# First stage of a two-layer backbone on one core: another split of the low halves between VectorE and GpSimd, other modulation pages, another order at the stage's end

## The chip, the core and the metric

The kernel runs on one core of a Trainium2 chip. The core has a matmul engine (TensorE, PE in the profile; its weight loads are listed as PEld), three engines for elementwise work (VectorE = DVE, ScalarE = ACT, GpSimd = POOL), a queue processor for loads (SyncE = SP) and 16 DMA engines. The metric is the device time of one execution in microseconds; smaller is better. The kernel before was timed three times: 1805.2, 1808.09 and 1814.19 us, median 1808.09.

## The reference, cut to what matters

Two layers work on 1024 latent tokens of width 1024, with 256 context tokens beside them: first windowed attention with 16 query heads and 4 key/value heads, then a Conformer convolution module. The change touches the start of the first layer only: the modulation vectors, the norm, and the first projections of the attention layer.

```python
shift, scale, gate = jnp.split((silu_c @ ada_w[i] + ada_b[i])[:, None, :], 3, axis=-1)
h_lat = modulate(rmsnorm(x, norm_g[i]), shift, scale)
shift_c, scale_c, gate_c = jnp.split(silu_cc @ ada_w[i] + ada_b[i], 3, axis=-1)
h_ctx = modulate(rmsnorm(h_ctx_stream, norm_g[i]), shift_c, scale_c)
...
proj = h_lat @ w_in
q = apply_rope(split_heads(proj[..., :q_end], N_Q_HEADS), cos, sin)
k = apply_rope(split_heads(proj[..., q_end:k_end], N_KV_HEADS), cos, sin)
v = split_heads(proj[..., k_end:v_end], N_KV_HEADS)
z = proj[..., v_end:]
kv_c = h_ctx @ w_in[:, q_end:v_end]
y = (o * jax.nn.silu(z)) @ w_out
```

## The kernel before

**Products.** An fp32 product A*B is made of three matmuls on rounded halves: high*high, low*high, high*low. A high half is a copy that ACT rounds, a low half is a subtraction (`split_lo`) on DVE or POOL. For weights the halves are called whi and wlo, made from the loaded page wraw; for the modulated latent tokens hh and hl, made from hf; for the context hch and hcl; for the modulation matrix ahi and alo, made from araw.

**The first stage** is written out instruction by instruction. `x` comes in as eight row tiles of 128 tokens, in two halves (`xs0`, `xs1`). ACT squares a row tile (`square`), `normalise` scales it on the engines that are listed, PE transposes it by 128 columns (`turn`), and `x_tiles` scales and shifts the result into hf and splits it. `x_mm(kt, half, acc, which)` multiplies the column tile `kt` of one half of the tokens by the weight chunks in `which` (0 = k, 1 = q of the first head, 2 = v), into PSUM. `acc0` and `acc1` are these sums for the two halves of the tokens; the third of `acc0` (v) and the first of `acc1` (k) are the two halves of one PSUM tile, `sb`. `c_tile` does for a context column tile what `turn` and `x_tiles` do for a latent one. `idle` issues matmuls of zeros.

**Modulation.** The modulation matrix is worked off in four blocks of four pages, `ada_load`, `ada_split`, `ada_mm` and `ada_cols` in this order. The pages in `ADA_FP` are multiplied in fp32 by the vector `cf`, without a split (in the profile one row of four passes, x4, for a page); the others as halves by `c4`, four matmuls. `ADA_G` names the pages whose low half POOL makes; the rest are DVE's. `ada_mm` copies the block's row to `arow`, and `ada_cols` turns it into the columns `mod` that `x_tiles` needs.

**Weights.** `WStream` loads chunks of 128 columns ahead into wraw; `wsA.split()` rounds the next one on ACT and subtracts on the engine that `lo_eng` gives. Chunk 3 is z, the gate of the first head.

**Order.** Each engine works through its own queue. While `pin("PVAG")` holds, PE, DVE, ACT and POOL keep the order of the program; after `pin("P")` only PE does, and the other engines' instructions are placed by the scheduler. Before the change, `pin("P")` stands at the very end of the stage, behind the ropes of both halves (`rope_start`: a copy on ACT, two DMAs on ACT's queue that swap the halves, a product on DVE; `rope_end`: a product on POOL, a sum on DVE, the rounded copy on ACT, the low half on POOL), the copy of v (`finish`), the context products (`gemm_ctx`) and the rounding of chunk 3. Then z's projection and the next q are put into a queue (`enqueue`), from which `fill(n)` issues n matmuls, and the attention begins.

All instructions of the engines are recorded by one helper, line 90, so the profile's rows are told apart by the names of their tiles.

Of the kernel before, what the change touches and what calls it, by code (L numbers as in the profile page):

```python
# [14 lines left out]
P = 128  # L15
# [17 lines left out]
ADA_FP = ((0, 0), (0, 1), (0, 2), (0, 3), (1, 3))  # L33
ADA_G = ((1, 0), (1, 1), (2, 0), (2, 1), (3, 0), (3, 1))
# [61 lines left out]
def backbone_kernel(  # L96
# [18 lines left out]
    pg = Pages(pgpool, 45, "page", 1024)  # L115
# [13 lines left out]
    def ps_o(i=None):  # L129
        if i is None:  # L130
            oflip[0] ^= 1
            i = oflip[0]
        return ps.tile([P, 512], F32, tag=f"o{i}", name=nm("pso"), bufs=1)
# [125 lines left out]
    chunks = []  # L259
# [15 lines left out]
    wsA = WStream(chunks, nraw=4, lo_eng=lambda i: V if i == 3 else G)  # L275
# [46 lines left out]
    def idle(n):  # L322
        o = sb[:, 512:1024]
        for _ in range(n):
            PE.matmul(o, zr[:, 0:P], zr, start=True, stop=True)
# [4 lines left out]
    tp = ps_g()  # L330
# [53 lines left out]
    def ada_split(pr, pages=range(4)):  # L384
        for i in pages:
            if (pr, i) not in ADA_FP:
                eng = G if (pr, i) in ADA_G else V
                raw = araw[pr][i]
                rv = raw.rearrange("p a b c -> p a (b c)")
                h, l = pg.alloc(F32R, [2, 512], "ahi"), pg.alloc(F32R, [2, 512], "alo")  # L390
                act(h, rv, AF.Copy)
                split_lo(eng, l, rv, h)
                pg.free(raw)
                araw[pr][i] = (h, l)

    ada_o = {}

    def ada_mm(pr, pages=range(4)):

        if 0 in pages:  # L400
            ada_o[pr] = ps_o(0)
        o = ada_o[pr]
        for i in pages:
            for k in range(2):
                if (pr, i) in ADA_FP:
                    r = araw[pr][i].rearrange("p a b c -> p a (b c)")
                    parts = [(cf, r)]
                else:
                    parts = [(c4, r) for r in araw[pr][i]]
                for n, (c, r) in enumerate(parts):  # L410
                    PE.matmul(o[0:4], c[:, 2 * i + k, :], r[:, k], start=i + k + n == 0,
                              stop=i + k == 4 and n == len(parts) - 1)
            pg.free(*(araw[pr][i] if len(parts) == 2 else (araw[pr][i],)))
        if 3 in pages:
            V.tensor_copy(R[pr][0:4, 0:512], o[0:4])

    def ada_cols(pr):

        rw, m = R.pop(pr), mods[pr]
        cps = ps_o(1)  # L420
        for i in range(4):
            PE.matmul(cps[:, 2 * i:2 * i + 2], rw[0:5, i * P:(i + 1) * P], sel[0:5], start=True, stop=True)
        hp.free(rw)
        with tc.high_priority():
            V.tensor_copy(m[:, 0:2], cps[:, 0:4].rearrange("p (a b) -> p a b", b=2))
            for i in range(2):
                V.tensor_scalar(out=m[:, 2 + i], in0=cps[:, 4 + 2 * i:6 + 2 * i], scalar1=1.0,
                                scalar2=vt[:, 96 + 2 * pr + i:97 + 2 * pr + i], op0=ALU.add, op1=ALU.mult)
# [53 lines left out]
    ada_mm(0, range(4))  # L482
    tps = [turn(xs0, kt, ps_g) for kt in range(2)]
    wsA.split()
# [4 lines left out]
    ada_split(1, range(2))  # L489
    x_tiles((tps[0], 0, 0, V), (tps[1], 1, 0, V))  # L490
    ada_split(1, range(2, 4))
# [5 lines left out]
    ada_mm(1)  # L497
# [7 lines left out]
    normalise(xs1, (V, A, V, V), lambda: x_tiles((tps[0], 2, 0, V), (tps[1], 3, 0, G)))  # L505
    idle(2)
    x_mm(2, 0, acc0, range(3))
    x_mm(3, 0, acc0, range(3))
    ada_split(2, range(2))
    tps = [turn(xs1, kt, ps_g) for kt in (0, 1)] + [turn(xs1, 2, lambda: ps_o(1))]  # L510
    ada_mm(2, range(1))
    x_tiles((tps[0], 0, 1, V), (tps[1], 1, 1, G))
    x_tiles((tps[2], 2, 1, V))
    ada_split(2, range(2, 4))
# [4 lines left out]
    t3 = turn(xs1, 3, lambda: ps_o(1))  # L519
    x_tiles((t3, 3, 1, G))  # L520
    ada_mm(2, range(1, 2))
    x_mm(1, 1, acc1, range(3))
    ada_mm(2, range(2, 4))
    x_mm(2, 1, acc1, range(3))
    ada_cols(2)
    tp = turn(xs0, 4, lambda: ps_o(0))
    x_mm(3, 1, acc1, (0,))
    tq = turn(xs1, 4, lambda: ps_o(1))
    x_tiles((tp, 4, 0, V), (tq, 4, 1, G))
    x_mm(3, 1, acc1, (1, 2))  # L530
    ada_split(3, range(2))
    tp = turn(xs0, 5, lambda: ps_o(0))
    tq = turn(xs1, 5, lambda: ps_o(1))
    x_tiles((tp, 5, 0, V), (tq, 5, 1, G))
# [8 lines left out]
    ada_mm(3)  # L543
    c_tile(ctodo.popleft(), 1)
    x_mm(5, 0, acc0, range(3))
    ada_cols(3)
    tp = turn(xs0, 6, lambda: ps_o(0))
    x_mm(5, 1, acc1, (0,))
    tq = turn(xs0, 7, lambda: ps_o(1))
    x_tiles((tp, 6, 0, V), (tq, 7, 0, G))  # L550
# [3 lines left out]
    tq = turn(xs1, 7, lambda: ps_o(1))  # L554
    x_mm(6, 0, acc0, range(3))
    x_tiles((tp, 6, 1, V), (tq, 7, 1, G))
    pg.free(*xs1)
    wsA.load()
# [8 lines left out]
    x_mm(7, 1, acc1, (0,))  # L567
    c_tile(ctodo.popleft(), 1)
    x_mm(7, 1, acc1, (1, 2))
# [518 lines left out]
    tails = [finish("v", 0, 0, acc0[2], d0[2])]  # L1088
    o = ps_o(0)
    run(gemm_ctx(wsA.hl[0], o))  # L1090
    rope_end(rk0, lo, *(t[:, lo] for t in d0[0]), V)
    finish("k", 0, 2, o, d0[0])
    rope_end(rq0, lo, *(t[:, lo] for t in d0[1]), V)
    o = ps_o(1)
    run(gemm_ctx(wsA.hl[2], o))
    rk1, rq1 = rope_start(acc1[0], hi), rope_start(acc1[1], hi, pg)
    tails.append(finish("v", 0, 1, acc1[2], d0[2]))
    tails.append(finish("v", 0, 2, o, d0[2]))
    rope_end(rk1, hi, *(t[:, hi] for t in d0[0]), V)
    rope_end(rq1, hi, *(t[:, hi] for t in d0[1]), V)  # L1100
    wsA.split()
# [4 lines left out]
    pin("P")  # L1106
# [3 lines left out]
    fill(8)  # L1110
    tails[0]()
    fill(8)
# [628 lines left out]
```

## Time and profile before

| | us |
|---|---|
| runs | 1805.2, 1808.09, 1814.19 |
| profiled execution | 1804.66 |
| its span on the core | 1802.9 |

The page gives the busy time of each engine and its share of the span. The views that the prediction reads are the windows (busy time of each engine in a stretch, then the granted clock of PE, the DMA share and GB/s), the waits (what PE waited for, with the total, the number and the longest), and the timeline (start, length, engine, line, operation, output<-inputs, and in brackets the idle time before with its releaser). Names of buffers stand without their numbers there. The second view of the page divides the span into 40 slices of 45 us and shows PE's busy share and clock in tenths:

```profile
PE   8859999989998999999999999999999999999997
PEclk9979999999999999999999999999999999999999
```

The first three slices are the stage of the change and its end; nearly all that follows has a nine.

### The profile page before, as it was taken

How to read it: one execution, taken by the hardware profiler on the slowest of the kernel's cores; microseconds unless marked ns; L12 is line 12 of the kernel's file. 1: busy time of each engine (PE TensorE's matmuls, PEld its weight loads, DVE VectorE, ACT ScalarE, POOL GpSimd, SP SyncE). 2: the span in 40 equal slices, each digit the busy share in tenths (PEclk: the TensorE clock that was granted, in tenths of full speed). 3: DMA queues.
4: the chain of work that ended last, by engine and by line, in shares of the span. 5: the costliest groups of instructions: out<-in, count | busy, mean ns of one | idle time of the engine just before them, and what ended most of it. 6: DMA issues, size and time to landing. Idle time of an engine off the chain costs nothing.

```text
span 1802.9 us, 23880 instructions
## 1 busy us (share of the span) xinstructions
PE 1736.4 (96%) x8418; PEld 1430.2 (79%) x8418; DVE 1144.6 (63%) x2063; ACT 864.0 (48%) x1407; POOL 952.2 (53%) x853
## 2 busy tenths in 40 slices
PE   8859999989998999999999999999999999999997
PEld 4648887878887888878888888888888888788886
DVE  4735564546634564546613339999999999967823
ACT  5434443444433453444623436665656565366731
POOL 3544666356645665554200137999988888131300
PEclk9979999999999999999999999999999999999999
DMA  9123443445423443324886643111020202376971
GB/s 325 60 71 89 148 143 86 121 122 158 129 85 120 146 146 105 122 86 135 292 281 236 237 133 99 54 35 48 24 88 30 82 30 72 111 252 224 338 270 47
DMA packets 195324, 242.45 MB, mean 134 GB/s; under 512 B 11798, under 2 KB 126790, under 8 KB 195204
## 3 DMA queue, kind: packets, MB, share of 16 engines
q1 hardware_dynamic: 188340, 230.09, 39.1%
q10 hardware_dynamic: 6864, 10.84, 2.6%
q8 instruction: 66, 1.08, 0.3%
q14 instruction: 54, 0.44, 0.1%
HBM read 188.70 MB, written 41.69 MB: 128 GB/s over the span
## 4 chain that ended last, share of the span: by engine, by line
PE 85%; DMA 5%; POOL 3%; DVE 3%; ACT 2%; issue 2%; SPq 1%; ACTq 0%; DVEq 0%; POOLq 0%
PE psg L90 44%; PE pss L90 22%; PE pso L90 20%; DMA rope_half<-rope_half 1%; DMA low_page<-in_conv_w_out_dram 1%; POOL rope_half L90 1%; DMA araw_page<-in_ada_w_dram 1%; DMA low_page<-in_attn_w_out_dram 1%; DMA ozd<-oz_half 1%; SPq L90 1%; DVE mask_page L90 0%; POOL wlo_page L90 0%; POOL p_page L90 0%; POOL low_page L90 0%; POOL ql_page L90 0%
## 5 line engine op out<-in xcount | busy, mean ns | idle before, releaser
L90 POOL TENSOR_TENSOR odd_half<-odd_half,prod_half 128x513 f32<-128x513 f32 (+2 forms) x252 | 313.4, 1251 | 23.6 <-ACT prod_half L90 10.3
L90 PE MATMUL psg<-hh_page,whi_page 128*128 128x512 f32 x608 | 244.6, 402 | 17.5 <-ACT whi_page L90 17.5
L90 PE MATMUL psg<-hh_page,wlo_page 128*128 128x512 f32 x608 | 242.7, 399 | 0.3 <-DVE wlo_page L90 0.3
L90 PE MATMUL psg<-hl_page,whi_page 128*128 128x512 f32 x608 | 242.6, 399 | 0.0
L90 POOL TENSOR_TENSOR wlo_page<-wraw_page,whi_page 128x1024 fp32r<-128x1024 f32 x73 | 180.2, 2470 | 110.6 <-ACT whi_page L90 92.0
L90 ACT ACTIVATE prod_half<-ubuf,dww 128x513 f32<-128x513 f32 (+2 forms) x252 | 165.1, 674 | 109.3 <-POOL odd_half L90 107.4
L90 PE MATMUL psg<-h2h_page,whi_page 128*128 128x512 f32 x464 | 184.1, 397 | 0.0
L90 PE MATMUL psg<-h2l_page,whi_page 128*128 128x512 f32 x464 | 182.6, 394 | 0.0
L90 PE MATMUL psg<-h2h_page,wlo_page 128*128 128x512 f32 x464 | 182.2, 393 | 0.0
L90 POOL TENSOR_SCALAR p_page<-p_page,sc 128x640 f32<-128x640 f32 (+1 forms) x128 | 101.0, 789 | 151.8 <-DVE sc L90 144.9
L90 DVE SCALAR_TENSOR_TENSOR pss<-ubuf,dww,pss 128x512 f32<-128x512 f32 (+3 forms) x270 | 172.9, 673 | 0.1
L90 DVE SCALAR_TENSOR_TENSOR pss<-ubuf,wsum,pss 128x512 f32<-128x512 f32 (+3 forms) x270 | 172.2, 673 | 0.2
L90 ACT ACTIVATE p_page<-p_page,sc 128x641 f32<-128x641 f32 (+1 forms) x128 | 102.9, 804 | 104.6 <-DVE sc L90 100.8
L90 PEld LDWEIGHTS psg<-hh_page,whi_page 128*128 128x128 f32 x608 | 116.7, 192 | 40.1 <-ACT whi_page L90 17.7
L90 DVE TENSOR_TENSOR ptlo<-pss,pthi 128x640 fp32r<-128x640 f32 (+1 forms) x144 | 103.4, 718 | 67.0 <-ACT pthi L90 66.0
L90 ACT ACTIVATE pthi<-pss 128x640 fp32r<-128x640 f32 (+1 forms) x144 | 88.6, 615 | 103.3 <-PE pss L90 96.1
L90 PEld LDWEIGHTS psg<-hh_page,wlo_page 128*128 128x128 f32 x608 | 116.2, 191 | 26.8 <-DVE wlo_page L90 1.0
L90 PEld LDWEIGHTS psg<-hl_page,whi_page 128*128 128x128 f32 x608 | 116.6, 192 | 21.2
L90 ACT ACTIVATE whi_page<-wraw_page 128x1024 fp32r<-128x1024 f32 x88 | 92.5, 1053 | 70.9 <-PE psg L90 27.6
L90 PE MATMUL pso<-h2h_page,wlo_page 128*128 128x512 f32 x304 | 119.9, 394 | 0.0
L90 PE MATMUL pso<-h2h_page,whi_page 128*128 128x512 f32 x304 | 119.6, 393 | 0.0
L90 PE MATMUL pso<-h2l_page,whi_page 128*128 128x512 f32 x304 | 119.5, 393 | 0.0
(256 smaller groups left out, 4103.4 us busy)
## 6 DMA issues: line engine op xcount, KB each, us to landing
wraw_page<-in_conv_w_in_dram SPq DMA_DIRECT2D x48, 512.0 KB
wraw_page<-in_attn_w_in_dram SPq DMA_DIRECT2D x40, 512.0 KB
wo_page<-in_attn_w_out_dram SPq DMA_DIRECT2D x32, 512.0 KB
wol_page<-wolA SPq DMA_DIRECT2D x32, 512.0 KB
wo_page<-in_conv_w_out_dram SPq DMA_DIRECT2D x32, 512.0 KB
wol_page<-wolC SPq DMA_DIRECT2D x32, 512.0 KB
rope_half<-rope_half ACTq DMA_DIRECT2D x76, 128.0 KB
araw_page<-in_ada_w_dram SPq DMA_DIRECT2D x32, 256.0 KB
```

The source lines that it names most:

```text
L90: r = f(*a, **k)
```

## The change

- `ADA_FP` gets the pages (1,2), (2,2) and (2,3); `ADA_G` loses the pages of blocks 1 and 3, so their low halves go to DVE. `lo_eng` gives the wlo of chunks 1 and 2 to DVE, and six `x_tiles` entries go from POOL to DVE. `ada_mm` counts its pages, so that they can come in any order.
- The written-out order of the first stage is changed at many places: `x_tiles` of the first two tiles stands ahead of the second `wsA.split()` and of `ada_split(1)`; two more idle matmuls; block 2's fp32 pages come first; `x_mm(5, 0)` and `x_mm(5, 1)` are cut up otherwise; `wsA.load()` (the load of z's weights) moves ahead of `x_mm(6, 0)`; all of `x_mm(7, 1)` moves behind the last `c_tile`.
- At the end, `wsA.split()` of chunk 3 moves ahead of everything but the start of the first ropes and the copy of v, then comes `pin("P")`, then `x_mm(7, 1)`, and the ropes and context products are written down in another order. `fill(12)` takes the place of `fill(8)` twice.

What stands in the engines' queues, at three places. The first is PE at the end of the stage: `pso<-ident,x` are the transposes of the last context tile, the rows with hh and hl the last `x_mm(7, 1)`, those with hch the first context product, `pss_158` is the tile `sb`. Before:

```order
L90 MATMUL pss_158<-hh_page_702,whi_page_247 128x512 [waits Activation_49]
L90 MATMUL pss_158<-hl_page_703,whi_page_247 128x512 [waits Pool_49]
L90 MATMUL pss_158<-hh_page_702,wlo_page_248 128x512
L90 MATMUL pso_809<-ident,x_page_471 128x128 [waits DVE_49]
L90 MATMUL pso_809<-ident,x_page_472 128x128
L90 MATMUL psg_475<-hh_page_702,whi_page_251 128x512
L90 MATMUL psg_475<-hl_page_703,whi_page_251 128x512
```

Now:

```order
L90 MATMUL pso_790<-ident,x_page_459 128x128 [waits DVE_49]
L90 MATMUL pso_790<-ident,x_page_460 128x128
L90 MATMUL pss_158<-hh_page_693,whi_page_247 128x512 [waits Activation_49]
L90 MATMUL pss_158<-hl_page_694,whi_page_247 128x512
L90 MATMUL pss_158<-hh_page_693,wlo_page_248 128x512
L90 MATMUL psg_463<-hh_page_693,whi_page_271 128x512
```

The first three products have moved behind the transposes, and the copy of v, which reads the other half of `pss_158`, now stands ahead of them in the program: the wait on ACT is for that copy.

The second place is ACT at the same end of the stage, from the copy of v (`vf_half<-pss_158`) on; `whi_page_945` before and `whi_page_834` now are the weights of z. Before:

```order
L90 ACTIVATE vf_half_857<-pss_158 128x512 [waits PE_49]
L90 ACTIVATE kh_page_836<-rope_half_845 128x512 [waits DVE_49]
L90 ACTIVATE kvc_page_838<-pso_859 128x256 [waits PE_49]
L90 ACTIVATE qh_page_839<-rope_page_852 128x512 [waits DVE_49]
L90 ACTIVATE rope_half_919<-pss_158 128x512 [waits DMAHW7_49,DMAHW6_49]
...
L90 ACTIVATE whi_page_1160<-wraw_page_960 128x1024 [waits DMAHW1_49]
L90 ACTIVATE kh_page_836<-rope_half_921 128x512 [waits DVE_49]
L90 ACTIVATE qh_page_839<-rope_page_928 128x512 [waits DVE_49]
L90 ACTIVATE whi_page_945<-wraw_page_742 128x1024 [waits DMAHW6_49]
```

Now:

```order
L90 ACTIVATE rope_page_825<-pss_157 128x512 [waits DVE_49,Pool_49]
...
L90 ACTIVATE vf_half_832<-pss_158 128x512 [waits PE_49]
L90 ACTIVATE whi_page_834<-wraw_page_716 128x1024 [waits DMAHW6_49,Pool_49]
L90 ACTIVATE kh_page_811<-rope_half_820 128x512 [waits DVE_49]
L90 ACTIVATE rope_half_891<-pss_158 128x512 [waits PE_49]
```

The rounding of z's weights went from the last place to the one right behind the copy of v.

The third place is DVE at the second modulation block, from the low halves of the first two token tiles (hl) on; `arow_half_111` is the row of the block, `mod_196` its columns. Before:

```order
L90 TENSOR_TENSOR hl_page_272<-hf_page_273,hh_page_271 128x512 [waits Activation_49]
L90 TENSOR_TENSOR hl_page_277<-hf_page_278,hh_page_276 128x512 [waits Activation_49]
L90 TENSOR_TENSOR alo_page_284<-araw_page_114,ahi_page_283 128x1024 [waits DMAHW2_49,DMAHW1_49,Activation_49]
L90 COPY arow_half_111<-pso_322 4x512 [waits PE_49]
L90 COPY mod_196<-pso_352 128x4 [waits PE_49]
```

Now:

```order
L90 TENSOR_TENSOR hl_page_265<-hf_page_266,hh_page_264 128x512 [waits Activation_49]
L90 TENSOR_TENSOR wlo_page_272<-wraw_page_109,whi_page_271 128x1024 [waits DMAHW4_49,Activation_49]
L90 TENSOR_TENSOR alo_page_276<-araw_page_112,ahi_page_275 128x1024 [waits DMAHW6_49,DMAHW5_49,Activation_49]
L90 TENSOR_TENSOR alo_page_280<-araw_page_113,ahi_page_279 128x1024 [waits DMAHW7_49,DMAHW0_49,Activation_49]
L90 COPY arow_half_111<-pso_318 4x512 [waits PE_49]
L90 TENSOR_TENSOR wlo_page_333<-wraw_page_126,whi_page_332 128x1024 [waits DMAHW7_49,Activation_49]
L90 COPY mod_196<-pso_346 128x4 [waits PE_49]
```

DVE has the wlo of chunk 1 (`wlo_page_272`) behind hl, and that of chunk 2 (`wlo_page_333`) behind the copy of the row.

The diff:

```diff
@@ -30,8 +30,8 @@
 NEG = -1.0e30
 TB = T // P
 
-ADA_FP = ((0, 0), (0, 1), (0, 2), (0, 3), (1, 3))
-ADA_G = ((1, 0), (1, 1), (2, 0), (2, 1), (3, 0), (3, 1))
+ADA_FP = ((0, 0), (0, 1), (0, 2), (0, 3), (1, 2), (1, 3), (2, 2), (2, 3))
+ADA_G = ((2, 0), (2, 1))
 FILL = 12
 DEFER = 6
 EARLY = 2
@@ -272,7 +272,7 @@
         if h % 4 == 3 and h + 1 < NH:
             add_chunk(("k", h // 4 + 1), wk[h // 4 + 1])
             add_chunk(("v", h // 4 + 1), wv[h // 4 + 1])
-    wsA = WStream(chunks, nraw=4, lo_eng=lambda i: V if i == 3 else G)
+    wsA = WStream(chunks, nraw=4, lo_eng=lambda i: V if i in (1, 2, 3) else G)
 
     NPR = KT // 2
     R = {}
@@ -393,14 +393,15 @@
                 pg.free(raw)
                 araw[pr][i] = (h, l)
 
-    ada_o = {}
+    ada_o, ada_n = {}, {}
 
     def ada_mm(pr, pages=range(4)):
 
-        if 0 in pages:
-            ada_o[pr] = ps_o(0)
+        if pr not in ada_o:
+            ada_o[pr], ada_n[pr] = ps_o(0), 0
         o = ada_o[pr]
         for i in pages:
+            ada_n[pr] += 1
             for k in range(2):
                 if (pr, i) in ADA_FP:
                     r = araw[pr][i].rearrange("p a b c -> p a (b c)")
@@ -408,16 +409,16 @@
                 else:
                     parts = [(c4, r) for r in araw[pr][i]]
                 for n, (c, r) in enumerate(parts):
-                    PE.matmul(o[0:4], c[:, 2 * i + k, :], r[:, k], start=i + k + n == 0,
-                              stop=i + k == 4 and n == len(parts) - 1)
+                    PE.matmul(o[0:4], c[:, 2 * i + k, :], r[:, k], start=ada_n[pr] == 1 and k + n == 0,
+                              stop=ada_n[pr] == 4 and k == 1 and n == len(parts) - 1)
             pg.free(*(araw[pr][i] if len(parts) == 2 else (araw[pr][i],)))
-        if 3 in pages:
+        if ada_n[pr] == 4:
             V.tensor_copy(R[pr][0:4, 0:512], o[0:4])
 
-    def ada_cols(pr):
+    def ada_cols(pr, bank=1):
 
         rw, m = R.pop(pr), mods[pr]
-        cps = ps_o(1)
+        cps = ps_o(bank)
         for i in range(4):
             PE.matmul(cps[:, 2 * i:2 * i + 2], rw[0:5, i * P:(i + 1) * P], sel[0:5], start=True, stop=True)
         hp.free(rw)
@@ -479,22 +480,21 @@
 
     square(xs0, range(4))
     normalise(xs0, (V, A, V, A))
-    ada_mm(0, range(4))
+    ada_mm(0)
     tps = [turn(xs0, kt, ps_g) for kt in range(2)]
-    wsA.split()
     wsA.split()
     ada_cols(0)
     acc0 = [sa[:, 0:512], sa[:, 512:1024], sb[:, 0:512]]
     acc1 = [sb[:, 512:1024]]
-    ada_split(1, range(2))
     x_tiles((tps[0], 0, 0, V), (tps[1], 1, 0, V))
-    ada_split(1, range(2, 4))
+    wsA.split()
+    ada_split(1)
     idle(8)
     for n in range(2):
         x_mm(0, 0, acc0, (n,))
         x_mm(1, 0, acc0, (n,))
     ada_load(3)
-    ada_mm(1)
+    ada_mm(1, (2, 3, 0, 1))
     wsA.split()
     square(xs1, (0, 1, 2))
     x_mm(0, 0, acc0, (2,))
@@ -502,36 +502,35 @@
     tps = [turn(xs0, kt, ps_g) for kt in (2, 3)]
     x_mm(1, 0, acc0, (2,))
     square(xs1, (3,))
-    normalise(xs1, (V, A, V, V), lambda: x_tiles((tps[0], 2, 0, V), (tps[1], 3, 0, G)))
-    idle(2)
+    x_tiles((tps[0], 2, 0, V), (tps[1], 3, 0, G))
+    idle(4)
+    normalise(xs1, (V, A, V, V))
     x_mm(2, 0, acc0, range(3))
     x_mm(3, 0, acc0, range(3))
-    ada_split(2, range(2))
+    ada_mm(2, (2,))
+    ada_split(2)
     tps = [turn(xs1, kt, ps_g) for kt in (0, 1)] + [turn(xs1, 2, lambda: ps_o(1))]
-    ada_mm(2, range(1))
-    x_tiles((tps[0], 0, 1, V), (tps[1], 1, 1, G))
+    ada_mm(2, (3,))
+    x_tiles((tps[0], 0, 1, V), (tps[1], 1, 1, V))
     x_tiles((tps[2], 2, 1, V))
-    ada_split(2, range(2, 4))
     cx = load_rows(ctx[0], 2)
     ctodo = deque(range(KT))
     acc1 += [ps_g(), ps_g()]
     x_mm(0, 1, acc1, range(3))
-    t3 = turn(xs1, 3, lambda: ps_o(1))
-    x_tiles((t3, 3, 1, G))
-    ada_mm(2, range(1, 2))
+    ada_mm(2, (0, 1))
+    tp = turn(xs1, 3, lambda: ps_o(1))
+    x_tiles((tp, 3, 1, V))
     x_mm(1, 1, acc1, range(3))
-    ada_mm(2, range(2, 4))
+    ada_cols(2, 0)
     x_mm(2, 1, acc1, range(3))
-    ada_cols(2)
     tp = turn(xs0, 4, lambda: ps_o(0))
-    x_mm(3, 1, acc1, (0,))
     tq = turn(xs1, 4, lambda: ps_o(1))
-    x_tiles((tp, 4, 0, V), (tq, 4, 1, G))
-    x_mm(3, 1, acc1, (1, 2))
+    x_tiles((tp, 4, 0, V), (tq, 4, 1, V))
     ada_split(3, range(2))
+    x_mm(3, 1, acc1, range(3))
     tp = turn(xs0, 5, lambda: ps_o(0))
     tq = turn(xs1, 5, lambda: ps_o(1))
-    x_tiles((tp, 5, 0, V), (tq, 5, 1, G))
+    x_tiles((tp, 5, 0, V), (tq, 5, 1, V))
     ada_split(3, range(2, 4))
     cos, sin = (pg.alloc(F32, [1024], n) for n in ("cos", "sin"))
     SY.dma_start(out=cos, in_=k_cos)
@@ -541,21 +540,23 @@
     normalise(cx, (V, G))
     x_mm(4, 1, acc1, range(3))
     ada_mm(3)
+    x_mm(5, 0, acc0, (0,))
     c_tile(ctodo.popleft(), 1)
-    x_mm(5, 0, acc0, range(3))
-    ada_cols(3)
+    x_mm(5, 0, acc0, (1, 2))
+    ada_cols(3, 0)
+    c_tile(ctodo.popleft(), 1)
+    x_mm(5, 1, acc1, (0,))
     tp = turn(xs0, 6, lambda: ps_o(0))
-    x_mm(5, 1, acc1, (0,))
     tq = turn(xs0, 7, lambda: ps_o(1))
-    x_tiles((tp, 6, 0, V), (tq, 7, 0, G))
+    x_tiles((tp, 6, 0, V), (tq, 7, 0, V))
     x_mm(5, 1, acc1, (1, 2))
     pg.free(*xs0)
     tp = turn(xs1, 6, lambda: ps_o(0))
     tq = turn(xs1, 7, lambda: ps_o(1))
+    wsA.load()
     x_mm(6, 0, acc0, range(3))
-    x_tiles((tp, 6, 1, V), (tq, 7, 1, G))
+    x_tiles((tp, 6, 1, V), (tq, 7, 1, V))
     pg.free(*xs1)
-    wsA.load()
     for i in range(2):
         c_tile(ctodo.popleft(), i)
     x_mm(7, 0, acc0, range(3))
@@ -564,9 +565,6 @@
     x_mm(6, 1, acc1, range(3))
     for i in range(2):
         c_tile(ctodo.popleft(), i)
-    x_mm(7, 1, acc1, (0,))
-    c_tile(ctodo.popleft(), 1)
-    x_mm(7, 1, acc1, (1, 2))
     hp.free(zr_pg)
 
     def rope_start(o, sl, pool=hp):
@@ -1086,30 +1084,32 @@
     lo, hi = slice(0, 512), slice(512, 1024)
     rk0, rq0 = rope_start(acc0[0], lo), rope_start(acc0[1], lo, pg)
     tails = [finish("v", 0, 0, acc0[2], d0[2])]
+    wsA.split()
+    pin("P")
+    x_mm(7, 1, acc1, range(3))
+    tails.append(finish("v", 0, 1, acc1[2], d0[2]))
     o = ps_o(0)
     run(gemm_ctx(wsA.hl[0], o))
     rope_end(rk0, lo, *(t[:, lo] for t in d0[0]), V)
+    rq1 = rope_start(acc1[1], hi, pg)
+    rope_end(rq0, lo, *(t[:, lo] for t in d0[1]), V)
     finish("k", 0, 2, o, d0[0])
-    rope_end(rq0, lo, *(t[:, lo] for t in d0[1]), V)
+    rk1 = rope_start(acc1[0], hi)
     o = ps_o(1)
     run(gemm_ctx(wsA.hl[2], o))
-    rk1, rq1 = rope_start(acc1[0], hi), rope_start(acc1[1], hi, pg)
-    tails.append(finish("v", 0, 1, acc1[2], d0[2]))
     tails.append(finish("v", 0, 2, o, d0[2]))
+    rope_end(rq1, hi, *(t[:, hi] for t in d0[1]), V)
     rope_end(rk1, hi, *(t[:, hi] for t in d0[0]), V)
-    rope_end(rq1, hi, *(t[:, hi] for t in d0[1]), V)
-    wsA.split()
     for i in range(3):
         wsA.done(i)
     wsA.nraw = 2
     wsA.load()
-    pin("P")
     enqueue(("z", 0))
     enqueue(("q", 1))
     load_vecs()
-    fill(8)
+    fill(12)
     tails[0]()
-    fill(8)
+    fill(12)
     scores(0, 0)
     for t in tails[1:]:
         fill(8)
```

## Prediction

> **What bounds the kernel now.** I read four views, coarse to fine. First the page: the span, the engines' busy time, the chain that ended last.
>
> ```profile
> span 1802.9 us, 23880 instructions
> PE 1736.4 (96%) x8418; PEld 1430.2 (79%) x8418; DVE 1144.6 (63%) x2063; ACT 864.0 (48%) x1407; POOL 952.2 (53%) x853
> PE 85%; DMA 5%; POOL 3%; DVE 3%; ACT 2%; issue 2%; SPq 1%; ACTq 0%; DVEq 0%; POOLq 0%
> ```
>
> TensorE (PE) is busy 1736.4 of 1802.9 us, so only some 66 us are not matmul time. Next the table by windows: after the time come PE, weight loads, DVE, ACT, POOL, the granted PE clock, and DMA.
>
> ```profile
> 0.00:25.00 25.00, 20.26 (x67) 10.99 (x67) 7.61 (x24) 15.66 (x23) 7.34 (x10) 1.00 0.97 304
> 25.00:50.00 25.00, 20.84 (x84) 12.53 (x85) 16.77 (x23) 11.70 (x18) 10.41 (x6) 0.86 0.96 319
> 50.00:75.00 25.00, 23.18 (x112) 15.15 (x110) 19.03 (x22) 11.54 (x17) 14.04 (x7) 1.00 0.17 54
> 75.00:100.00 25.00, 22.91 (x139) 19.32 (x139) 12.45 (x26) 7.07 (x14) 11.32 (x14) 1.00 0.15 40
> 100.00:125.00 25.00, 7.21 (x26) 5.31 (x26) 6.72 (x9) 9.73 (x15) 14.67 (x13) 0.59 0.37 98
> 125.00:150.00 25.00, 24.07 (x130) 20.35 (x129) 14.51 (x34) 9.58 (x20) 4.95 (x8) 1.00 0.19 53
> ```
>
> The hole is 100 to 125 us: PE busy 7.21 of 25 us at a clock of 0.59. It is the end of the stage that the change rewrites. From 125 us on PE is busy 24.07 of 25, so what the stage gains should reach the end. Third, PE's waits in the first 300 us (total, times, longest):
>
> ```profile
> PE psg L90 <- ACT whi_page L90: 17.5, 1, 17.5
> PE pss L90 <- DVE hl_page L90: 4.0, 3, 1.9
> PE pss L90 <- ACT hh_page L90: 1.6, 1, 1.6
> PE pso L90 <- POOL alo_page L90: 1.5, 2, 0.8
> PE pso L90 <- DVE x_page L90: 1.3, 1, 1.3
> PE pso L90 <- DVE alo_page L90: 1.2, 1, 1.2
> ```
>
> One wait holds 17.5 us; the others that the change touches make 9.6 together. Last, PE's timeline (start, length, operands; in brackets the wait and its releaser):
>
> ```profile
> 20.16 2.11 PE L90 MATMUL pss<-zr_half 128*128 128x512 f32 x8
> 23.86 0.49 PE L90 MATMUL pss<-hh_page,whi_page 128*128 128x512 f32 x1 [1.58 <-ACT hh_page L90]
> 26.26 0.50 PE L90 MATMUL pss<-hl_page,whi_page 128*128 128x512 f32 x1 [1.91 <-DVE hl_page L90]
> 29.04 0.79 PE L90 MATMUL pss<-hl_page,whi_page 128*128 128x512 f32 x1 [1.81 <-DVE hl_page L90]
> 30.05 0.63 PE L90 MATMUL pss<-hh_page,whi_page 128*128 128x512 f32 x1
> 30.48 0.63 PE L90 MATMUL pss<-hl_page,whi_page 128*128 128x512 f32 x1
> 36.30 1.88 PE L90 MATMUL pso<-araw_page,cf 128*4 128x512 f32 x4
> 38.12 0.50 PE L90 MATMUL pss<-hh_page,whi_page 128*128 128x512 f32 x1
> 43.57 0.40 PE L90 MATMUL pss<-hh_page,whi_page 128*128 128x512 f32 x1
> 43.80 0.40 PE L90 MATMUL pss<-hl_page,whi_page 128*128 128x512 f32 x1
> 47.02 1.04 PE L90 MATMUL psg<-ident,x_page 128*128 128x128 f32 x8
> 74.75 0.40 PE L90 MATMUL pso<-alo_page,c 128*4 128x512 f32 x1
> 93.23 0.44 PE L90 MATMUL pso<-ident,x_page 128*128 128x128 f32 x2 [0.17 <-DVE hf_page L90]
> 94.90 0.28 PE L90 MATMUL pso<-hch_page,whi_page 128*128 128x256 f32 x1
> 100.42 0.28 PE L90 MATMUL pso<-hch_page,wlo_page 128*128 128x256 f32 x1
> 118.22 0.80 PE L90 MATMUL psg<-hh_page,whi_page 128*128 128x512 f32 x1 [17.52 <-ACT whi_page L90]
> ```
>
> A 512-column matmul starts every 0.23 us (43.57 to 43.80) at full clock and every 0.43 (30.05 to 30.48) at half. These rows cut the stage into the stretches that I price.
>
> **The change part by part**, each stretch from its row before to its row after.
>
> *(a) From the idle matmuls (end 22.27) to the end of the second modulation block (38.12, where the next product starts): 15.9 us.* Work at full clock: 12 products (2.8), three split pages of four matmuls (12 x 0.23 = 2.8) and one fp32 page (1.88). Only 7.4 is work; 5.3 is the three waits, the rest half clock. The waits come from these rows:
>
> ```profile
> 23.84 5.14 DVE L90 TENSOR_TENSOR hl_page<-hf_page,hh_page 128x512 fp32r<-128x512 f32 x2 [1.71 <-ACT hh_page L90]
> 23.30 5.13 POOL L90 TENSOR_TENSOR alo_page<-araw_page,ahi_page 128x1024 fp32r<-128x1024 f32 x2
> 42.25 0.69 DVE L90 TENSOR_TENSOR hl_page<-hf_page,hh_page 128x512 fp32r<-128x512 f32 x1
> 118.20 1.45 DVE L90 TENSOR_TENSOR wlo_page<-wraw_page,whi_page 128x1024 fp32r<-128x1024 f32 x1 [1.64 <-ACT whi_page L90]
> ```
>
> Two subtractions of DVE took 5.14 us while POOL ran its own two; one with POOL idle took 0.69. After the change POOL has nothing between its first weight page and a late row tile, the ACT copies of the two tiles stand ahead of the modulation copies, and so the first two waits go. What is late next is the second weight page's wlo, now on DVE behind both tile subtractions: about 1.4 us of wait (1.45 for the page itself). One split page becomes fp32: 1.88 for 0.92. So 7.4 + 1.0 + 1.4 = 9.8; 0.2 off since the first products overlap the idle ones. **Gain 6.3.**
>
> The Trainium skill, "SBUF — State Buffer", section "Who interferes with whom", has a DVE instruction with two SBUF inputs and a GpSimd instruction that reads SBUF lock one port, and the later one fully blocked. The trace agrees: 5.14 beside 5.13. By that rule moving POOL's subtractions to DVE costs less than their own sum, and by the same rule one that still meets POOL waits out a whole POOL instruction; the second is the slower rival below.
>
> *(b) To the end of the fourth tile's products (47.02): 8.9 us.* Two more idle matmuls (0.46). The third weight page's wlo is now behind the DVE copy of the modulation row, which waits for block (a): 0.3 + 0.68 for the copy + 1.45, against two products ready: a new wait of 1.7; 0.5 of small waits go. Queued behind it on PE is everything, on DVE the modulation columns, which had a round trip there anyway. **Loss 1.7.**
>
> *(c) To the end of the last modulation block (75.15): 28.1 us,* of which waits 3.1, work 25.0. Two more pages in fp32: +1.9. The low halves of the last four modulation pages are all on DVE now (two were POOL's), as are the tile subtractions. From the fourth tile pair on DVE has 4 x 0.77 (scaling) + 4 x 0.69 + 4 x 1.45 + gaps 0.6 = 12.3 us, PE ahead of the last page 27 products, 8 transposes and 12 modulation matmuls = 9.7: a wait of about 2.5. So 25.0 + 1.9 + 2.5 = 29.4. **Loss 1.3** (0 to 3: DVE's speed decides).
>
> *(d) To the last context transposes (93.23): 18.1 us.* Three products (0.7) go behind the stage's end; 1.3 of the row tile's wait shrinks, since a product of the sixth tile now stands ahead of it. **Gain 1.6.** Sum of (a) to (d): 4.9. If half of (b)'s new wait were there in (c) anyway (DVE, done with wlo early, would be ahead by as much), it would be 5.8 to 6.5; I take 5.7, and the last transposes at 87.5.
>
> *(e) From there to the gate's first product.* Before: 118.22 - 93.23 = 25.0, and this product then ran at half clock, 0.43 for 0.23, until about 122.8: 2.3 more, and 0.3 wait for wlo, 27.6 in all. Cause:
>
> ```profile
> 98.43 0.60 ACT L90 ACTIVATE rope_page<-pss 128x512 f32<-128x512 f32 x1 [2.61 <-DVE rope_half L90]
> 100.26 0.60 ACT L90 ACTIVATE vf_half<-pss 128x512 f32<-128x512 f32 x1 [1.24 <-POOL rope_half L90]
> 116.59 0.63 ACT L90 ACTIVATE qh_page<-rope_page 128x512 fp32r<-128x512 f32 x1 [3.32 <-DVE rope_page L90]
> 117.13 1.99 ACT L90 ACTIVATE whi_page<-wraw_page 128x1024 fp32r<-128x1024 f32 x2
> ```
>
> The gate's rounding stood last on ACT, behind both ropes. Now it stands right after the copy of v (100.26), so its whi is there at about 103.5 - 93.2 = 9 us after the transposes and its wlo at 10.4: early. But a **new wait** comes: three of the nine products of the last tile write the PSUM tile whose first half that copy of v reads. Before, they ran ahead of it (93.42 on); now PE holds them until v is copied, 100.86 - 93.23 = 7.6 us after the transposes, and behind them both context GEMMs and the gate. So: transposes 0.4 + idle 7.6 + nine products 2.1 + context GEMMs 5.8 (94.90 to 100.70) + half clock after the idle 2.2 = 18.1. The rope rows that the gate's bank needs are done at about 12.8, sooner. **Gain 27.6 - 18.1 = 9.5.**
>
> On the clock, the Trainium skill, "TensorE: Matmul & The Clock Gate", section "What's actually happening", says that half clock follows an idle window of about 3.4 us and ends after as much sustained work. By that the spell costs 1.7 and not 2.2; the trace's spell after 118.22 lasted 4.6 us, so the measurement decides.
>
> *(f) The fill of 12 for 8* lets matmuls of the same queue run ahead; PE's order is the same from the fourth head on: nothing. POOL's freed time and 3 ACT roundings are off the path: nothing. The gate's weight load is issued ahead of one tile's products and still early; if it were late, ACT's rounding would hold the vf-to-gate chain, whose slack is 18.1 - 10.4 = 7.7.
>
> Sum: 5.7 + 9.5 = 15.2. The profiled execution took 1804.66 us: 1789.5. The median of the runs, 1808.09, lies 0.19% above it; 1792.9 on that scale. **Forecast 1790 us**, its own range 1784 to 1797.
>
> **The rivals.**
> - *Only the end gains:* loads or DVE set the early pace, so (a) is eaten in (c). For: DMA share 0.97 and 0.96 in the first 50 us. Against: PE's early waits name DVE and ACT. 1804.7 - 9.5 = 1795. Chance 0.14.
> - *Only the early part gains:* the new wait on v grows, when ACT's rope copies come later than before (they wait on DVE's rope rows, 2.61, which wait on a load). 1804.7 - 5.7 = 1799. Chance 0.14, half of it within 0.5%.
> - *More:* the hole closes to bare work (no half clock, early waits all gone): 1780. Chance 0.06.
> - *Slower: DVE becomes the bound in (c).* Twelve subtractions move from POOL to DVE. If each meets POOL as the rows of 23.84 did, a 128x512 costs 2.57 for 0.69 and a page 2.8 (the row below), for 1.45: 6 x 1.9 + 6 x 1.4 = 19.6 us; with three spells of half clock at 2.3 the time is 1789.5 + 19.6 + 6.9 = 1816, 1819 at the median's scale. It decides from 15 us of stretch. Against: POOL keeps only four of its instructions in the stretch. Chance 0.05.
>
> ```profile
> 68.58 5.65 DVE L90 TENSOR_TENSOR alo_page<-araw_page,ahi_page 128x1024 fp32r<-128x1024 f32 x2
> ```
>
> - *The change doesn't do what it says:* by the table three pages are new in fp32, not four (two blocks' pages move, one leaves POOL otherwise), which is in the sum. That nothing at all passes on, since later stages wait for loads instead: 1805. Chance 0.04.
>
> **How the numbers follow.** The forecast has 0.57. The range 1782 to 1801 takes in the first two rivals and leaves out the last three, 0.15, and a little of the forecast's tails. A measurement tells about 0.5% (9 us) from no change, so faster is below 1799: 0.57 + 0.14 + 0.07 + 0.06 = 0.84; same 0.07 + 0.04 + 0.01 = 0.12; slower 0.04.
>
> **What would show it.** In the profile after: the first products with tile subtractions of 0.7 us and no wait over 2 us before 32 us; the transposes of the last context tile near 87.5; a PE wait of about 7.6 us named for ACT's v copy ahead of the last tile's products, then the gate's first product near 105.5 without a wait on whi. A wait for alo on DVE over 4 us before 75 us would show (c) mis-sized; a wait on rope rows ahead of the gate would show (e) wrong; and a PE busy share under 24 of 25 us behind 125 us that the stage's gain was given back.

## The result, and the profile after

| | us |
|---|---|
| six runs, changed kernel | 1792.5 to 1796.51, median 1795.28 |
| six runs, kernel before | 1800.7 to 1814.19, median 1806.8 |
| ratio | 0.9932, 95% interval 0.9908 to 0.9956 |
| spans of the two profiled executions | 1794.1 and 1802.9 |

The change made the kernel faster by 0.68%, about 12 us on the median before, with an interval from 8 to 17 us; the two profiled spans differ by 8.8 us. The forecast's own sum was a gain of 15.2 us; its 1790 us, set beside the first median of 1808.09, amounts to 18. Each ratio below is to the kernel before as timed beside that run (medians 1806.8, 1808.84 and 1807.8 us). By the page after, PE is busy 1738.5 of 1794.1 us.

The windows of the first 125 us, with the columns of the table before:

```profile
0.00:25.00 25.00, 21.60 (x73) 12.12 (x74) 8.24 (x26) 13.78 (x21) 3.33 (x8) 1.00 0.96 302
25.00:50.00 25.00, 23.21 (x95) 12.22 (x94) 15.49 (x25) 13.12 (x20) 6.05 (x3) 1.00 0.97 321
50.00:75.00 25.00, 22.66 (x111) 15.19 (x109) 16.49 (x28) 10.03 (x16) 1.61 (x2) 1.00 0.20 64
75.00:100.00 25.00, 17.52 (x89) 14.48 (x89) 14.34 (x25) 9.87 (x18) 10.32 (x12) 0.86 0.20 50
100.00:125.00 25.00, 23.42 (x137) 20.11 (x136) 10.12 (x23) 10.75 (x19) 14.88 (x16) 1.00 0.38 104
```

The hole of 100 to 125 us is gone (PE busy 23.42 us for 7.21). A smaller one stands in 75 to 100 us. PE's timeline names it; these rows answer to those of the prediction:

```profile
20.96 2.12 PE L90 MATMUL pss<-zr_half 128*128 128x512 f32 x8
25.85 0.50 PE L90 MATMUL pss<-hh_page,wlo_page 128*128 128x512 f32 x1 [0.30 <-DVE wlo_page L90]
32.35 0.40 PE L90 MATMUL pss<-hh_page,whi_page 128*128 128x512 f32 x1
34.41 0.49 PE L90 MATMUL pss<-hh_page,wlo_page 128*128 128x512 f32 x1 [1.43 <-DVE wlo_page L90]
42.92 1.88 PE L90 MATMUL pso<-araw_page,cf 128*4 128x512 f32 x4
68.52 0.39 PE L90 MATMUL pso<-alo_page,c 128*4 128x512 f32 x1 [0.32 <-DVE alo_page L90]
70.36 0.40 PE L90 MATMUL pss<-hh_page,whi_page 128*128 128x512 f32 x1
87.35 0.60 PE L90 MATMUL pso<-ident,x_page 128*128 128x128 f32 x4
95.42 0.79 PE L90 MATMUL pss<-hh_page,whi_page 128*128 128x512 f32 x1 [7.48 <-ACT vf_half L90]
105.25 0.39 PE L90 MATMUL psg<-hh_page,whi_page 128*128 128x512 f32 x1
```

The last context transposes stand at 87.35, the new wait on the copy of v takes 7.48 us, and the gate's first product starts at 105.25 at full clock. Before it started at 118.22 and lost 2.6 us more behind that, so the stage gave 15.6 us. But the span gained 8.8. The loss is behind the stage: PE's waits between 150 and 330 us (the first group of four heads), first of the kernel before, then of the changed one.

```profile
PE pss L90 <- POOL p_page L90: 2.7, 1, 2.7
PE pss L90 <- DVE ptlo L90: 1.4, 2, 0.9
PE pss L90 <- DVE sc L90: 0.3, 1, 0.3
```

```profile
PE pss L90 <- POOL p_page L90: 3.9, 3, 2.0
PE pso L90 <- ACT pthi L90: 3.5, 1, 3.5
PE pss L90 <- DVE sc L90: 1.1, 2, 0.9
PE pss L90 <- DVE ptlo L90: 0.9, 1, 0.9
PE pso L90 <- DVE ptlo L90: 0.6, 2, 0.4
```

4.4 us before, 10.0 after. The names in these rows are those of the softmax chain (masked scores, probabilities, their halves), which projection matmuls from the queue are meant to cover. The prediction had named the sign of this, a stretch behind 125 us with PE busy under 24 of 25 us: 250 to 275 us now has 20.09, where it had 24.68 before (275 to 300: 22.17 for 21.40).

### The profile page after: what moved, and what is told of

It reads as the page before. It is cut to its first block, busy times and chain, and to the rows that moved or that the text cites. A ratio compares the mean times of both kernels' runs of the same rounds, so it can differ in the third digit from the quotient of the medians.

```text
span 1794.1 us, 23861 instructions
## 1 busy us (share of the span) xinstructions
PE 1738.5 (97%) x8420; PEld 1430.6 (80%) x8420; DVE 1142.1 (64%) x2072; ACT 862.3 (48%) x1404; POOL 927.7 (52%) x841
## 4 chain that ended last, share of the span: by engine, by line
PE 86%; DMA 5%; DVE 2%; ACT 2%; POOL 2%; issue 1%; ACTq 0%; SPq 0%; POOLq 0%; DVEq 0%
PE psg L90 44%; PE pss L90 22%; PE pso L90 21%; DMA rope_half<-rope_half 1%; DMA low_page<-in_conv_w_out_dram 1%; DMA low_page<-in_attn_w_out_dram 1%; POOL rope_half L90 1%; DMA ozd<-oz_half 1%; DMA rope_page<-rope_page 0%; DMA araw_page<-in_ada_w_dram 0%; DVE mask_page L90 0%; ACT pthi L90 0%; POOL low_page L90 0%; DMA wo_page<-in_conv_w_out_dram 0%; DVE ptlo L90 0%
## 5 line engine op out<-in xcount | busy, mean ns | idle before, releaser
L90 POOL TENSOR_TENSOR wlo_page<-wraw_page,whi_page 128x1024 fp32r<-128x1024 f32 x71 | 175.0, 2466 | 111.2 <-ACT whi_page L90 91.7
```

The source lines that it names most:

```text
L90: r = f(*a, **k)
```

## The experiments

Two theories stood for the 6 us or so lost between the gate and the second group of heads: A, the fill of 12 runs eight matmuls ahead that are then missing at the end of the first group of heads; B, the other engines' instructions are placed otherwise, as PE alone is in fixed order earlier. Besides these, the prediction's terms were taken apart.

**Fill 8 again in the changed kernel.**

```diff
-    fill(12)
+    fill(8)
     tails[0]()
-    fill(12)
+    fill(8)
```

> The changed kernel with the two fills of 12 back at 8. The stage's gain at the gate's first product was 15 us, but the span is only 8.8 shorter, and by the first regroup of heads (about 320 us) the lead has sunk from 14.9 to 9.3. Theory A (fill): the eight matmuls run ahead are missing at the end of the first group of heads, where nothing else covers the waits; with 8 the lead stays 14 to 15 behind 350 us and the time is about 1790. Rival B (placement): the other engines' instructions in the attention are placed otherwise by the scheduler since PE alone is in fixed order earlier; then the lead sinks again to about 9 and the time stays 1794 to 1796.

Median 1793.24 us, ratio to the kernel before 0.9921 (0.9906 to 0.9936), not the 1790 that theory A expected. The runs can't tell it from the changed kernel (0.9932), the trace does: PE's waits of 150 to 330 us are 4.9 us,

```profile
PE pss L90 <- POOL p_page L90: 2.7, 1, 2.7
PE pss L90 <- DVE ptlo L90: 1.2, 2, 0.9
PE pss L90 <- DVE sc L90: 1.0, 3, 0.4
```

and from the gate's first product to the first output of head 4 it takes 228.8 us, where the changed kernel takes 234.7 (and the kernel before 231.0, with the 2.6 us that it lost behind the gate's start). That is 6.0 us for A in this stretch, and 4.4 of them are left at the end of the span. With fill 8 the stretch is 0.3 us longer than before without those 2.6, so that is what rival B can have cost in these profiles. The lead at that output was 13.4 us, not quite the 14 to 15 expected.

**Fill 12 in the kernel before.** The same two lines the other way.

> The kernel before with the two fills of 8 at 12, nothing else. Theory A: 3 to 5 us slower than before, all of it between 250 and 330 us (about 1811). Rival B: no change (1805 to 1809).

Median 1812.03, ratio 1.0021 (1.0006 to 1.0037), 3.8 us slower. The waits of 150 to 330 us, 8.7 in all, have the names and lengths of the changed kernel's, in a kernel that has none of its other edits:

```profile
PE pso L90 <- ACT pthi L90: 3.5, 1, 3.5
PE pss L90 <- POOL p_page L90: 2.5, 2, 2.0
PE pss L90 <- DVE ptlo L90: 1.1, 2, 0.9
PE pss L90 <- DVE sc L90: 0.9, 1, 0.9
PE pso L90 <- DVE ptlo L90: 0.7, 2, 0.4
```

From the gate's first product to the first output of head 4 it takes 235.3 us for 231.0. A is shown by both runs; B is left with the 0.3 us above.

**Fewer matmuls per step in the first group of heads** (with fill 8):

```diff
-            fill(FILL)
+            fill(FILL if h > 3 else FILL - 1)
```

> The changed kernel with fill 8, and 11 in place of 12 matmuls of projection in each step of the first four heads, so that the queue lasts to their end. Theory A (the queue that runs dry is what makes the waits near 270 to 285 us): those waits (3.5 us in all) shrink to under 1 and the time falls by 2 to 4 us against fill 8. Rival: the waits are those of the softmax chain itself and come in each step once fewer matmuls cover it; no change or slower.

Median 1790.43, ratio 0.9905 (0.9888 to 0.9922); the waits of 150 to 330 us shrink to 2.1 us, 1.7 of them on GpSimd's p_page, and those between 262 and 300 us from 3.6 to 0.2. The waits go as theory A has it; the time, 3 us less, can't be told from fill 8.

**The new end alone**, behind the old first stage (fill 8): the old stage without its last `x_mm(7, 1)`, then the changed lines from `d0 =` on.

> The stage of the kernel before up to its last context tile, with the new end (rounding of the gate's weights first, all nine products of the last tile behind the copy of v, only PE in fixed order); fill 8. The prediction's step (e) gives 9.5 us: gate's first product at about 111, and 1797 if nothing is lost behind it. If the parts need each other, under 6 us.

Median 1799.35, ratio 0.9948 (0.9934 to 0.9961): 9.4 us, as step (e) had it; the gate's first product at 111.35.

**The new first stage alone**, with the old end (fill 8; all of `x_mm(7, 1)` ahead of the first rope).

> The new first stage (low halves on VectorE, three more fp32 pages, new order) with the old end (all four engines in fixed order up to the gate's rounding); fill 8. The prediction's steps (a) to (d) give 5.7 us: last context transposes at 87.4, gate's first product near 112 to 113, the time about 1801. If DMA or the start's scatter sets the early pace, no gain (1806).

Median 1800.29, ratio 0.9955 (0.9942 to 0.9969), 8.1 us for 5.7 expected; the gate's first product at 113.2, 5.0 sooner than before. The two parts are 17.5 us by their ratios and 14.3 together with fill 8; each has an interval of about 2.5 us to either side, so the difference is not clear of noise.

**The low halves back on GpSimd**, with the new order and the new pages (fill 8):

```diff
-ADA_G = ((2, 0), (2, 1))
+ADA_G = ((1, 0), (1, 1), (2, 0), (2, 1), (3, 0), (3, 1))
-lo_eng=lambda i: V if i in (1, 2, 3) else G
+lo_eng=lambda i: V if i == 3 else G
-    x_tiles((tps[0], 0, 1, V), (tps[1], 1, 1, V))
+    x_tiles((tps[0], 0, 1, V), (tps[1], 1, 1, G))
...
```

> The changed kernel with fill 8 and the twelve subtractions back on GpSimd (two weight pages, six token tiles, four modulation pages); order and fp32 pages as changed. Theory: in the first 35 us VectorE's two tile subtractions again last as long as GpSimd's beside them (5 us for 1.4), PE waits for them, the last context transposes come 4 to 6 us later than 64.4 us after the first product, and the time rises by as much. Rival: the early gain is the new order's alone (the copies of the two tiles ahead of the modulation copies); then under 2 us.

Median 1792.29, ratio 0.9925 (0.9905 to 0.9944): no difference to the same kernel with them on VectorE (0.9921). The theory fell. DVE's two tile subtractions take 1.41 us here too:

```profile
22.26 1.41 DVE L90 TENSOR_TENSOR hl_page<-hf_page,hh_page 128x512 fp32r<-128x512 f32 x2
```

```profile
18.68 2.37 POOL L90 TENSOR_TENSOR wlo_page<-wraw_page,whi_page 128x1024 fp32r<-128x1024 f32 x1 [17.23 <-ACT whi_page L90]
23.97 2.41 POOL L90 TENSOR_TENSOR wlo_page<-wraw_page,whi_page 128x1024 fp32r<-128x1024 f32 x1 [2.92 <-ACT whi_page L90]
```

POOL (second view) has nothing to do between 21.05 and 23.97, since the new order makes ACT copy the tiles first, and just there DVE's subtractions fall. There they no longer meet. PE's waits only change places: it waits 1.51 us for the second weight page's wlo on GpSimd and not for v's, where the changed kernel waits 0.30 and 1.43.

**The old order of the copies, low halves on VectorE** (fill 8):

```diff
     wsA.split()
+    wsA.split()
     ada_cols(0)
...
+    ada_split(1, range(2))
     x_tiles((tps[0], 0, 0, V), (tps[1], 1, 0, V))
-    wsA.split()
-    ada_split(1)
+    ada_split(1, range(2, 4))
```

> The changed kernel with fill 8, and at the first two token tiles the order of the kernel before: second weight chunk and two modulation pages rounded ahead of the tiles' copies; low halves stay on VectorE. Theory (the early gain is this order's, not the engine's, as the run with the low halves on GpSimd said): VectorE now has a weight page and two modulation pages ahead of the tiles, PE waits 4 to 6 us more for the first products, and the time rises by 4 to 8 us. Rival: the order is indifferent as long as GpSimd is quiet; under 1 us.

Median 1799.13, ratio 0.9955 (0.9937 to 0.9972), 6 us slower than the same kernel with the new order. PE's first product waits, and the products behind it run at half clock, 0.42 us apart (PE first, then VectorE):

```profile
20.30 2.14 PE L90 MATMUL pss<-zr_half 128*128 128x512 f32 x8
26.21 0.50 PE L90 MATMUL pss<-hh_page,whi_page 128*128 128x512 f32 x1 [3.77 <-ACT hh_page L90]
...
27.96 0.63 PE L90 MATMUL pss<-hh_page,whi_page 128*128 128x512 f32 x1
28.38 0.63 PE L90 MATMUL pss<-hl_page,whi_page 128*128 128x512 f32 x1
```

```profile
20.46 1.72 DVE L90 TENSOR_TENSOR wlo_page<-wraw_page,whi_page 128x1024 fp32r<-128x1024 f32 x1 [1.37 <-ACT whi_page L90]
...
22.43 2.35 DVE L90 TENSOR_TENSOR alo_page<-araw_page,ahi_page 128x1024 fp32r<-128x1024 f32 x2
24.69 1.52 DVE L90 TENSOR_SCALAR hf_page<-psg,mod 128x512 f32<-128x512 f32 x2
```

VectorE scales the two tiles (hf) only behind a weight page and two modulation pages, as the theory had it. So the old order loses on either engine, but not in the same way: with the low halves on GpSimd, VectorE's two tile subtractions last 5.14 us beside GpSimd's (in the prediction); with them on VectorE, they take 1.41 us but the tiles come late.

With this the four corners are there. From the end of the idle matmuls to the last context transposes, in the profiles:

| | lows on GpSimd | lows on VectorE |
|---|---|---|
| old order of the copies | 71.0 (kernel before), 76.2 (the same with fill 12) | 70.2 (this run) |
| new order | 64.3 | 64.3 (changed kernel: 23.08 to 87.35) |

The upper left corner also has the old order in the rest of the stage and three pages fewer in fp32, and its two profiles differ by 5.2 us. This run's 70.2 has about 1 us of half clock in it that the new order's 64.3 have not (granted clock 0.66 from 40 to 45 us). So the upper row is told by runs: the old stage with the new end has 0.9948, this run 0.9955, the same within noise. The new order alone brings the early gain (lower left); the other engine alone brings none that the runs can tell (upper right).

**The low half of v's weights on GpSimd alone** (fill 8):

```diff
-lo_eng=lambda i: V if i in (1, 2, 3) else G
+lo_eng=lambda i: V if i in (1, 3) else G
```

> The changed kernel with fill 8 and the low half of v's weights alone back on GpSimd, which is idle there. Theory: the 1.4 us wait of PE for it near 35 us goes (GpSimd ends it 2.4 us after the rounding, before the modulation block does), and the last context transposes come 1 to 1.5 us sooner; too small for the median to tell. Rival: it meets VectorE's subtractions of the modulation pages and lengthens those; no gain.

Median 1793.99, ratio 0.9928 (0.9909 to 0.9947). PE's wait of 1.43 us at 34 us is gone, and still the last transposes come 65.9 us after the idle matmuls for 64.3: the windows behind 70 us show half clock there, first this run, then the changed kernel.

```profile
70.00:75.00 5.00, 3.70 (x12) 2.56 (x13) 1.69 (x3) 0.42 (x1) 2.24 (x2) 0.71 0.00 0
75.00:80.00 5.00, 5.00 (x22) 4.45 (x23) 2.16 (x7) 0.71 (x2) 0.73 (x1) 0.60 0.00 0
```

```profile
70.00:75.00 5.00, 3.03 (x14) 1.82 (x11) 2.87 (x9) 0.85 (x4) 1.61 (x2) 1.00 0.24 73
75.00:80.00 5.00, 5.00 (x34) 4.36 (x34) 3.18 (x8) 1.49 (x3) 1.45 (x2) 1.00 0.02 6
```

Both have the same two waits there (1.4 and 0.6 us, on the row tiles); only one got the slow spell. The rival's longer subtractions are not there: VectorE's first pair of modulation pages takes 2.36 us for 2.35.

**The last tile's products ahead of the copy of v** (fill 8), so that nothing in `sb` holds them:

```diff
+    x_mm(7, 1, acc1, range(3))
     hp.free(zr_pg)
...
     pin("P")
-    x_mm(7, 1, acc1, range(3))
```

> The changed kernel with fill 8, and the nine products of the last tile written ahead of the copy of v, so that nothing in PSUM holds them; the gate's rounding stays early. Theory: the 7.5 us wait of PE on the copy of v is the price of the new order; without it the gate's first product comes 10 to 12 us after the last context transposes (17.9 with it), held by its own rounding, and the time falls 5 to 7 us against the same kernel with the wait (about 1787). Rival: the ropes or the gate's weights set that moment anyway (VectorE, DMA); then it comes no earlier than 16 us and the time does not move.

Median 1786.32, ratio 0.9882 (0.9862 to 0.9902), 7 us faster than with the wait. The gate starts at 98.1, 8.9 us after the last transposes and sooner than the 10 to 12 expected. The other engines' order changes with it too, and VectorE makes the gate's low half later (10.0 us after the transposes for 9.0). PE's waits from 85 to 125 us that touch the gate are

```profile
PE psg L90 <- DVE wlo_page L90: 2.7, 1, 2.7
...
PE psg L90 <- ACT whi_page L90: 0.5, 1, 0.5
```

**The row that waits for the sink's load, later** (fill 8): the line that makes `nsink` moved behind the ropes; on DVE it then stands behind the first rope product.

> The changed kernel with fill 8, and the small row on VectorE that waits for the sink's load (3.3 us) behind the first rope product instead of ahead of it. Theory: the 7.5 us wait of PE for the copy of v is the tail of a chain sink load, that row, first rope product, second rope copy on ACT, copy of v; with the row behind the product ACT gets on 2 to 2.5 us sooner and PE's wait is 5 to 5.5 us; the time falls by about 2 us, which the median can hardly tell. Rival: ACT's own DMA issues (1.2 and 1.1 us, between its copies) set it; then the wait stays over 7.

Median 1791.4, ratio 0.9919 (0.9893 to 0.9944). PE's wait for the copy of v is 6.2 us for 7.5. ACT's timeline (ACTq: its DMA issues) shows the rest of the chain:

```profile
91.65 1.16 ACTq L90 DMA_DIRECT2D rope_half<-rope_half  x2
92.91 0.60 ACT L90 ACTIVATE rope_page<-pss 128x512 f32<-128x512 f32 x1 [1.29 <-DVE rope_half L90]
93.58 1.12 ACTq L90 DMA_DIRECT2D rope_page<-rope_page  x2
94.75 0.60 ACT L90 ACTIVATE vf_half<-pss 128x512 f32<-128x512 f32 x1 [1.24 <-issue]
```

The wait ahead of the second copy fell from 2.61 to 1.29 us, so the sink's load was 1.3 us of PE's wait, less than the 2 to 2.5 expected. Now each gap between ACT's copies is about the length of the DMA issues in it, as the rival had it, though the wait did not stay over 7.

**Two edits together**: the products ahead of the copy of v, and 11 matmuls per step.

> Two of the edits that were measured alone, together: the last tile's products ahead of the copy of v, and 11 matmuls of projection per step in the first four heads (first fills of 8). The first was worth 7 us beside fill 8 (ratio 0.9882 against 0.9921), the second 3 us (0.9905). If they add, the ratio to the kernel before is about 0.987 (1784); if the queue of 344 matmuls is used otherwise once the gate starts 9 us earlier, the second gives nothing and it stays 0.988.

Median 1780.2 us (1776.27 to 1782.91), ratio 0.9856 (0.9834 to 0.9878), the fastest of the study: 1.44% under the kernel before, where the change has 0.68%. The two add, as 0.987 had it; the rival's 0.988 lies just outside the interval.

**The gate's rounding ahead of the ropes too.**

> As the two edits together, and the rounding of the gate's weights ahead of the first ropes as well (with it, the row that waits for the sink's load stands behind the gate's low half on VectorE). Theory: the 0.5 and 2.7 us waits of PE on the gate's whi and wlo go, and with them the half clock behind them (6 products at 0.43 us for 0.23); the gate starts without a wait at the end of the context products, and the time falls 3 to 4 us more, to a ratio of about 0.985 (1781). Rival: the ropes come 2 us later and the first scores wait for q and k instead; then no gain.

Median 1781.47, ratio 0.9868 (0.9845 to 0.9891): nothing gained. The waits on whi and wlo are gone, and a new one is there, 85 to 125 us:

```profile
PE pso L90 <- ACT vf_half L90: 5.9, 1, 5.9
```

PE now reaches the transposes of v before ACT has copied it; the rival was right in kind, with v in the place of q and k.

## Why the prediction was right, and where it was off

- *The number alone shows little.* 1795.28 us lies in the range, but it is also what the first rival gave (1795, only the end gains). The trace and the runs tell the two apart: the early part alone gave 8.1 us. In the profiles, the scale of the sum, 1789.5 was forecast and 1795.88 measured. The median of the runs is nearer to what the sum gives on that scale, 1792.9.
- *The end, step (e): right.* 17.9 us from the last transposes to the gate (18.1 predicted), the wait on v 7.48 (7.6), gate at 105.25. The end alone gave 9.4 us by runs for 9.5. That this wait was the price of the order was shown by taking it away: 7 us. Two slips of the sum did no harm. Its 7.6 us start with the transposes, whose 0.4 it adds again; v's copy ended 8.0 us after their start, which hid that. And 103.5 - 93.2 is 10.3 and not 9; a rounding of 1.05 behind the copy of v gives 8.7, and whi was there at 9.0.
- *Step (a): right in size, not in its parts.* Idle matmuls to the end of the second block took 9.3 us for 9.6. But the wait for the second page's wlo, 1.4 in the sum, was 0.30, with eight products ahead of it on PE, and the rest took 0.8 more than the sum has: the two nearly cancel. I gave GpSimd's absence and the copies' order as joint reasons; the corners show that the order does it alone. GpSimd is also not idle up to the row tile, as (a) says: it subtracts for a token tile at 38.90 us and for two modulation pages at 43.09, behind (a)'s stretch.
- *Step (b): right.* 10.6 us, with the wait for v's wlo at 1.43 for the 1.7 estimated. The terms given for that wait add up to 2.0; the subtraction took 1.20 us for the 1.45 among them.
- *Step (c): mis-sized.* 27.4 us for 29.4. The wait on DVE's last modulation pages, 2.5 us in the sum, was 0.32 and under 0.3. DVE's pair of modulation pages took 2.36 us (its timeline below) for the 2.9 that I had from the row of the gate's wlo, a row that ran in part beside a GpSimd subtraction (117.30 to 118.57). That is 1.1 of the 2 us for the four pages; the rest was not taken apart. So (c) gained 0.7 in place of losing 1.3.

```profile
67.24 2.36 DVE L90 TENSOR_TENSOR alo_page<-araw_page,ahi_page 128x1024 fp32r<-128x1024 f32 x2 [0.26 <-ACT ahi_page L90]
```

- *Step (d): 17.0 for 16.5.* Together (a) to (d) put the last transposes at 87.35 for 87.5. That it is so close is luck in part: the idle matmuls ended 0.8 us later than before, and from there it is 64.3 us for a forecast of 65.2.
- *Step (f) failed:* "nothing" for the fill of 12. PE's order is the same from the second group of heads on, much as it said, but a queue that ends at a fixed place pays for each matmul taken early. The kernel before with that edit alone lost 3.8 us. In the changed kernel it cost 6 us by the profiles up to head 4. By the medians it is 2 us, with overlapping intervals: with fill 8 the gain is 14.3 us, close to the 15.2 of the sum, with fill 12 it is 12. The rest of the distance to 18 is that 1790 was set beside a median 3.4 us above the profiled execution.
- *The rivals.* The wait on v that I feared would eat the end's gain stayed at its size. DVE did not become the bound, with GpSimd's subtractions or without. That the gain is given back behind the stage was in none of the rivals as a mechanism, only among the signs to look for; a part of it was.

## What to carry to other kernels

When a change moves work earlier out of a queue that fills gaps, count how many pieces are left for the last gaps before the queue is refilled. When two halves of one PSUM tile go to different readers, a write to one half may be made to wait for a reader of the other, here for 7.5 us: order the writes ahead of the reads (a tile for each was not tried here). And when an engine seems slow since another runs beside it, test the order of their work before moving it: here the order alone was worth about 6 us by the runs, and the other engine alone nothing that they can tell.

## What the runs showed of the hardware that was not expected

- *The half clock comes or stays away for the same waits.* 1.4 and 0.6 us of wait near 71 us cost one run a spell from 72 to 79 us at 0.43 us per product, and the changed kernel nothing. The edit that took 1.4 us of wait away so ended 1.6 us later. The kernel before and the same kernel with fill 12, alike up to the gate, both wait 1.3 and 0.6 us at this place; only the second has a spell behind it (its windows below, granted clock 0.66), and lost 3.1 us. Of ten profiles with the new order, seven need 64.3 us from the idle matmuls to the last context transposes; the three that need 65.4 to 65.9 are those with such a spell. The Trainium skill, "TensorE: Matmul & The Clock Gate", section "What's actually happening", says that the activity window runs freely, so that the point where the clock changes depends on where in the window the work falls. That would allow such a difference; no run here shows where the window lies, and the cause stays open.

```profile
80.00:85.00 5.00, 4.52 (x16) 3.40 (x16) 0.57 (x2) 0.42 (x1) 1.16 (x2) 0.66 0.00 0
85.00:90.00 5.00, 5.00 (x22) 4.27 (x22) 2.48 (x7) 0.98 (x2) 0.00 (x0) 0.66 0.00 0
```

- *The start scatters by more than the edit.* These two profiles have the gate's first product at 118.22 and 124.36. 0.9 us of the difference is there at the end of the idle matmuls (23.21 in the second). 2.1 us come up to the end of the second block, where VectorE's two tile subtractions beside GpSimd's took 7.45 us for 5.14 (rows of the second below). The other 3.1 us are the spell. Between two profiles, stretches are to be compared from a mark inside, with an eye on the granted clock, and totals by runs.

```profile
24.82 7.45 DVE L90 TENSOR_TENSOR hl_page<-hf_page,hh_page 128x512 fp32r<-128x512 f32 x2 [1.76 <-ACT hh_page L90]
99.41 0.44 PE L90 MATMUL pso<-ident,x_page 128*128 128x128 f32 x2 [0.17 <-DVE hf_page L90]
```
